# Attention pipeline with its steps set further apart, transposes alternating between two whole PSUM banks

## The chip, the cores and the metric

The kernel runs on one core of one Trainium2 chip. The metric is the device time of one execution in microseconds (us). The engines are named as the profile names them: PE is TensorE, PEld its weight load, DVE VectorE, ACT ScalarE, POOL GpSimd and SP SyncE.

## The reference

One layer of a decoder over 256 tokens of width 2048, all in float32. The part that matters here is the attention and the projections on either side of it:

```python
h = rms_norm(x, mix_norm_g)
q, kv, gate_logits, conv_in = split(h @ w_in)          # 16 query heads, 4 key/value heads, head size 64
# three branches, each a softmax over logits + T5 bias, each weighted by a sigmoid gate:
#   compressed: keys/values squeezed to 15 blocks by a small MLP
#   selected:   top-16 blocks of 64 (all 4 blocks here, so all causal keys)
#   window:     last 512 keys (all causal keys here)
attn = g0 * o_cmp + g1 * o_sel + g2 * o_win
conv = conformer_conv(conv_in)                          # GLU, 31 taps, LayerNorm, swish
x = x + concat([attn, conv]) @ w_out
x = x + conv_glu_ffn(rms_norm(x))                       # 2048 -> 2 x 5632 -> 2048, 3 taps
return rms_norm(x, final_norm_g)
```

## The kernel before, in words

Every float32 product of weights is computed as three products of rounded parts: a weight chunk (128 x 2048) arrives in `wraw`, ACT rounds it into `wh` (line 110), DVE or POOL forms the rest `wl` (line 115), and PE adds high x high, high x low and low x high in PSUM (`mm3`, lines 144 to 146, for the input projections; `mm_rows`, lines 151 to 153, for the output projections).

The order of the instructions on each engine is the order in which the program is written. While PE works on a chunk, `hook` is called four times at even distances. It may call `attn_tick`, then runs what stands in `behind`, issues one piece of the next weight split (`w_pump`), and runs one entry of the list `steps`.

The input projection ends with eight tiles of queries (`i` = 0 to 7, 48 `mm3` matmuls each, in bank 0 or 1 by turns). When a tile is done, `q_evac` (line 659, DVE) scales it, and `q_split` splits it into a high half (line 665, ACT) and a low half (line 666, DVE). Behind it runs a software pipeline over 32 units; unit n is one pair (head slot, branch), four units to a query tile, and odd and even units share one score product. One call of `attn_tick` is one tick and issues each step for a different unit:

- `st_scores`: PE, logits of two units (lines 732 and 733), into bank 2 and bank 4 or 5
- `st_min`: DVE, adds the bias, writes `e` and its minimum `mn` (line 742)
- `st_exp`: ACT, exponential of `e` with sums into `lsum` (line 753)
- `st_rec`: DVE, reciprocal and gate (lines 761 and 762), once for two units
- `st_scale`: POOL, scales `e` (line 768)
- `st_transpose`: PE, three 128 x 128 transposes of `e` into bank 6 (line 774)
- `st_evac`: ACT, copies bank 6 to `es` (line 779)
- `st_out`: PE, every fourth unit, the products with the values into the lower half of bank 7 (lines 794 and 797); ACT then rounds the result to `ma_h` (line 798) and DVE forms `ma_l` (line 799)

The table at line 815 says how many ticks back the unit of each step lies: scores 0, min 1, exp 1, reciprocal and scale 3, transposes and eviction 5, output 6. Within a tick the steps are issued in the order of the table.

The compressed branch runs beside it from the list `steps`, for two query tiles at a time: `cmp_scores` (PE, line 678, bank 3), `cmp_exp` (DVE lines 688 to 692, ACT line 693), `cmp_probs` (DVE lines 698 to 701), `cmp_tr` (PE, two transposes at line 706 in bank 3 again, ACT copy to `pct` at line 708).

The first tick falls into query tile 1; tiles 2 to 7 have four ticks each, and 12 of the 38 ticks fall into the first three of the 16 chunks of the output projection, which reads `ma_h` and `ma_l`. From there to the end PE runs the rest of the output projection, the up projection (lines 1000 and 1002) and the down projection.

## Time and profile before

| | us |
|---|---|
| median of three runs (1119.32 to 1121.04) | 1120.76 |
| profiled execution | 1119.51 |
| its span, first to last instruction | 1117.7 |
| PE busy | 1098.8 |
| DVE busy | 768.4 |
| ACT busy | 577.0 |
| POOL busy | 187.8 |

The profiled execution is one run with its own time; its span is 1.8 us shorter, which lies before the first and after the last instruction. Busy times are sums over the whole span, so they say nothing about a single stage. In an order of time a number after an instruction says how long its engine had stood idle just before it, and the arrow names what ended that.

### The profile page before, as it was taken

How to read it: one execution, taken by the hardware profiler on the slowest of the kernel's cores; microseconds unless marked ns; L12 is line 12 of the kernel's file. 1: busy time of each engine (PE TensorE's matmuls, PEld its weight loads, DVE VectorE, ACT ScalarE, POOL GpSimd, SP SyncE). 2: the span in 40 equal slices, each digit the busy share in tenths (PEclk: the TensorE clock that was granted, in tenths of full speed). 3: DMA queues.
4: the chain of work that ended last, by engine and by line, in shares of the span. 5: the costliest groups of instructions: out<-in, count | busy, mean ns of one | idle time of the engine just before them, and what ended most of it. 6: DMA issues, size and time to landing. Idle time of an engine off the chain costs nothing.

```text
span 1117.7 us, 16341 instructions
## 1 busy us (share of the span) xinstructions
PE 1098.8 (98%) x6530; PEld 957.2 (86%) x6530; DVE 768.4 (69%) x1255; ACT 577.0 (52%) x833; POOL 187.8 (17%) x143
## 2 busy tenths in 40 slices
PE   8999999998999999999999999999999999999997
PEld 8999999886788888888888888888888888888885
DVE  7899976766356677777777777777778655556554
ACT  7534456777645554555455555545555444444442
POOL 0888756666100000000000000000000000000000
PEclk9999999999999999999999999999999999999999
DMA  9685426222464655555555555555555555555542
GB/s 375 235 294 198 170 79 246 94 80 86 175 226 155 230 188 196 188 193 191 192 191 194 190 190 190 189 188 189 188 189 189 189 188 188 189 183 188 186 158 76
DMA packets 32425, 207.46 MB, mean 186 GB/s; under 512 B 3883, under 2 KB 6203, under 8 KB 8284
## 3 DMA queue, kind: packets, MB, share of 16 engines
q1 hardware_dynamic: 28972, 199.85, 49.9%
q10 hardware_dynamic: 3376, 6.55, 1.6%
q8 instruction: 51, 0.84, 0.3%
q14 instruction: 26, 0.21, 0.1%
HBM read 204.27 MB, written 2.12 MB: 185 GB/s over the span
## 4 chain that ended last, share of the span: by engine, by line
PE 92%; DVE 2%; ACT 2%; issue 1%; DMA 1%; POOL 1%; SPq 0%; POOLq 0%; DVEq 0%; ACTq 0%
PE bank L1000 29%; PE bank L1002 14%; PE bank L153 10%; PE bank L151 9%; PE bank L152 9%; PE bank L144 5%; PE bank L146 5%; PE bank L145 5%; PE bank L794 1%; DVE wl L115 1%; DMA hb<-in_head 1%; POOL e L768 1%; ACT wh L110 1%; ACT e L753 1%; PE bank L774 0%
## 5 line engine op out<-in xcount | busy, mean ns | idle before, releaser
L110 ACT ACTIVATE wh<-wraw 128x2048 fp32r<-128x2048 f32 (+2 forms) x239 | 355.6, 1505 | 366.7 <-issue 149.8
L115 DVE TENSOR_TENSOR wl<-wraw,wh 128x2048 fp32r<-128x2048 f32 (+1 forms) x185 | 363.9, 1973 | 197.2 <-ACT wh L110 197.1
L1000 PE MATMUL bank<-xt,wh 128*128 128x512 f32 x1408 | 488.7, 394 | 0.0
L1002 PE MATMUL bank<-xt,wl 128*128 128x256 f32 x1408 | 390.1, 277 | 0.0
L1000 PEld LDWEIGHTS bank<-xt,wh 128*128 128x128 f32 x1408 | 264.0, 188 | 61.2
L1002 PEld LDWEIGHTS bank<-xt,wl 128*128 128x128 f32 x1408 | 264.4, 188 | 0.0
L144 PE MATMUL bank<-xt,wh 128*128 128x256 f32 x512 | 146.8, 287 | 1.6 <-ACT wh L245 1.6
L146 PE MATMUL bank<-xt,wl 128*128 128x256 f32 x512 | 145.1, 283 | 0.3 <-DVE wl L246 0.2
L145 PE MATMUL bank<-xt,wh 128*128 128x256 f32 x512 | 144.8, 283 | 0.0
L152 PE MATMUL bank<-wl,gh 128*128 128x512 f32 (+1 forms) x360 | 140.8, 391 | 0.0
L151 PE MATMUL bank<-wh,gh 128*128 128x512 f32 (+1 forms) x360 | 140.8, 391 | 0.0
L153 PE MATMUL bank<-wh,gl 128*128 128x512 f32 (+1 forms) x360 | 140.8, 391 | 0.0
L180 POOL TENSOR_TENSOR rstd<-ms,half 128x1 f32<-128x1 f32 x4 | 2.2, 552 | 821.4 <-DVE ms L173 821.4
L115 POOL TENSOR_TENSOR wl<-wraw,wh 128x1024 fp32r<-128x1024 f32 (+1 forms) x54 | 121.4, 2284 | 31.0 <-ACT wh L110 27.3
L144 PEld LDWEIGHTS bank<-xt,wh 128*128 128x128 f32 x512 | 97.7, 191 | 3.5 <-ACT wh L245 2.1
L146 PEld LDWEIGHTS bank<-xt,wl 128*128 128x128 f32 x512 | 97.8, 191 | 0.7 <-DVE wl L246 0.7
L145 PEld LDWEIGHTS bank<-xt,wh 128*128 128x128 f32 x512 | 97.8, 191 | 0.4
L375 DVE SCALAR_TENSOR_TENSOR bank<-us,cw,bank 128x256 f32<-128x256 f32 x232 | 93.9, 481 | 2.0 <-ACT bank L370 1.6
L963 DVE SCALAR_TENSOR_TENSOR yt<-u,vecs,yt 128x255 f32<-128x255 f32 (+1 forms) x176 | 80.9, 480 | 3.1
L151 PEld LDWEIGHTS bank<-wh,gh 128*128 128x128 f32 x360 | 67.8, 188 | 15.8
L152 PEld LDWEIGHTS bank<-wl,gh 128*128 128x128 f32 x360 | 67.8, 188 | 15.8
L153 PEld LDWEIGHTS bank<-wh,gl 128*128 128x128 f32 x360 | 67.8, 188 | 15.8
(182 smaller groups left out, 1034.1 us busy)
## 6 DMA issues: line engine op xcount, KB each, us to landing
wraw<-in_w_u SPq DMA_DIRECT2D x88, 1024.0 KB, 4.8
wraw<-in_w_d SPq DMA_DIRECT2D x44, 1024.0 KB, 4.8
wraw<-in_w_t SPq DMA_DIRECT2D x30, 1024.0 KB, 5.1
wraw<-in_w_o SPq DMA_DIRECT2D x16, 1024.0 KB, 4.8
wraw<-in_w_vg SPq DMA_DIRECT2D x4, 608.0 KB, 3.9
hb<-in_head SPq DMA_DIRECT2D x2, 1024.0 KB, 9.7
xr<-in_x SPq DMA_DIRECT2D x2, 1024.0 KB, 19.1
wb<-rel_scratch ACTq DMA_DIRECT2D x1, 2048.0 KB, 10.3
```

The lines of the kernel that those rows point to most:

```text
L110: nc.scalar.activation(h[:, sl], raw[:, sl], AF.Copy)
L115: (nc.gpsimd if pooled else nc.vector).tensor_sub(l[:, sl], raw[:, sl], h[:, sl].bitcast(F32))
L144: nc.tensor.matmul(ps, wh, xh, start=first, stop=False)
L145: nc.tensor.matmul(ps, wh, xl, start=False, stop=False)
L146: nc.tensor.matmul(ps, wl, xh, start=False, stop=last)
L151: nc.tensor.matmul(ps, xh, wh, start=first, stop=False)
L152: nc.tensor.matmul(ps, xh, wl, start=False, stop=False)
L153: nc.tensor.matmul(ps, xl, wh, start=False, stop=last)
L375: nc.vector.scalar_tensor_tensor(y[:, j] if last else acc[0], us[:, j, k:k + T], cw[:, j, k:k + 1], acc[0], op0=OP.mult, op1=OP.add)
L963: nc.vector.scalar_tensor_tensor(ys[i][:, d:], us_[i][:, :T - d], fcw[:, c, k:k + 1], ys[i][:, d:], op0=OP.mult, op1=OP.add)
L1000: nc.tensor.matmul(bk[i], wh[:, k, sl], xt[:, kt].rearrange("p a t -> p (a t)"), start=kt == 0, stop=False)
L1002: nc.tensor.matmul(bk[i][:, :T], wl[:, k, sl], xt_h[:, kt], start=False, stop=kt == KD - 1)
```

## The change

Ticks: a unit's exponential is now issued two ticks after its scores instead of one, reciprocal and scale four ticks instead of three, the transposes six instead of five, the eviction `es` seven instead of five, the output product eight instead of six. The rounding of the output, which stood in the same tick as the output product, becomes two steps: `st_high` (ACT) one tick after it and `st_low` (DVE) two ticks after it; only the last unit has both at once.

Banks: the transposes of even units go to bank 3, of odd units to bank 6. The compressed branch leaves bank 3: its logits go to bank 1 and its transposes to bank 0, which are the query banks not being filled at that moment; for the last two query tiles, which fall into the output projection, to the upper half of bank 7 and to bank 5.

Queries: `q_split` issues the high half only; the low half (`q_low`) runs at the next hook. Ticks in the output projection are dealt out again: 40 ticks in all, 14 of them after the query tiles. `e` has six buffers instead of five and `es` five instead of four; two small tiles share the buffers of others.

```diff
-            if not side:
-                while behind:
-                    behind.pop(0)()
+            due, first = behind[:], not side
+            behind.clear()
+            for f in due if first else ():
+                f()
             w_pump(1)
             step()
             fill(1.0 if i in ticks else 0.8 if cbst["q"] else 2.0)
-            while behind:
-                behind.pop(0)()
+            for f in () if first else due:
+                f()
...
-            cf["d"] = wk.tile([P, 2, P], F32, name="dg", bufs=1)
+            cf["d"] = wk.tile([P, 2, P], F32, name="dg", tag="sg")
...
-            cm[kv] = hd = wk.tile([P, 4, 32], F32, name="hd")
+            cm[kv] = hd = wk.tile([P, 4, 32], F32, name="hd", tag="q32")
...
         def q_split(i):
             for r in range(2):
+                h = slice(64 * r, 64 * r + 64)
+                nc.scalar.activation(qs[h, i % 4, r], q32[i][h], AF.Copy)
+            behind.append(lambda: q_low(i))
+
+        def q_low(i):
+            for r in range(2):
                 h, o = slice(64 * r, 64 * r + 64), slice(64 - 64 * r, 128 - 64 * r)
-                nc.scalar.activation(qs[h, i % 4, r], q32[i][h], AF.Copy)
                 nc.vector.tensor_sub(qs[o, i % 4, r], q32[i][h], qs[h, i % 4, r].bitcast(F32))
...
-            cm["b"] = bank[3]
+            cm["b"] = bank[1] if m < 3 else bank[7][:, T:]
...
-            pg = cm["b"]
+            pg = bank[0] if m < 3 else bank[5]
...
-                        (cmp_scores, cmp_exp, lambda m: None, cmp_probs, cmp_tr))]
+                        (lambda m: None, cmp_scores, cmp_exp, cmp_probs, lambda m: None, cmp_tr))]
...
-            e = wk.tile([P, 384], F32, name="e", bufs=D_T)
+            e = wk.tile([P, 384], F32, name="e", bufs=6)
...
+        def st_pt(n):
+
+            return bank[6 if n % 2 else 3][:, :384]
+
         def st_transpose(n):
-            e = US[n][0]
-            pt = bank[6]
+            e, pt = US[n][0], st_pt(n)
...
-            es = wk.tile([P, 384], F32, name="es", bufs=4)
-            nc.scalar.activation(es, bank[6][:, :384], AF.Copy)
+            es = wk.tile([P, 384], F32, name="es", bufs=5)
+            nc.scalar.activation(es, st_pt(n), AF.Copy)
...
-            nc.scalar.activation(ma_h[:, i], bank[7][:, :T], AF.Copy)
-            nc.vector.tensor_sub(ma_l[:, i], bank[7][:, :T], ma_h[:, i].bitcast(F32))
+            if n == NU - 1:
+                st_high(n)
+                st_low(n)
+
+        def st_high(n):
+            if n % 4 == 3:
+                nc.scalar.activation(ma_h[:, n // 4], bank[7][:, :T], AF.Copy)
+
+        def st_low(n):
+            if n % 4 == 3:
+                nc.vector.tensor_sub(ma_l[:, n // 4], bank[7][:, :T], ma_h[:, n // 4].bitcast(F32))
...
-        DEEP = D_T + 1
+        DEEP = 8
...
-            for f, d in ((st_out, DEEP), (st_transpose, D_T), (st_scores, 0), (st_rec, D_S), (st_min, 1),
-                         (st_evac, D_T), (st_scale, D_S), (st_exp, 1)):
-                if 0 <= n - d < NU:
+
+            for f, d in ((st_out, DEEP), (st_transpose, 6), (st_scores, 0), (st_low, 10), (st_rec, 4), (st_min, 1),
+                         (st_evac, 7), (st_high, 9), (st_scale, 4), (st_exp, 2)):
+                if 0 <= n - d < NU - (f in (st_high, st_low)):
...
-        TICKS = {0: {}, 1: {2: 1, 3: 1}, 2: {0: 1, 1: 1, 2: 1, 3: 1}, 3: {0: 1, 1: 2, 2: 1, 3: 2}, 4: {1: 1, 2: 1, 3: 2}}
+        TICKS = {0: {}, 1: {2: 1, 3: 1}, 2: {0: 1, 1: 1, 2: 1, 3: 1}, 3: {0: 1, 1: 1, 2: 2, 3: 2}, 4: {0: 1, 1: 1, 2: 1}}
...
-                    hook(2 * t + k // 2, TICKS[(3, 4, 2)[min(n, 2)]])
+                    hook(2 * t + k // 2, TICKS[(3, 2, 4)[min(n, 2)]])
```

ACT's order in query tile 5, before: `qs` is the high half of the queries, `wh` a weight piece, `es` the eviction of the transposes, `e` the exponentials, `pct` the compressed branch, `ma_h` the rounded output (bank_67 is bank 3, bank_70 bank 6, bank_71 bank 7).

```order
L665 ACTIVATE qs<-q_2840 64x256 x2
L110 ACTIVATE wh<-wraw 128x1024
L779 ACTIVATE es<-bank_70 128x384
L753 ACTIVATE e,lsum<-e,mn 128x128
L753 ACTIVATE e,lsum<-e,mn 128x256
L110 ACTIVATE wh<-wraw 128x1024
L779 ACTIVATE es<-bank_70 128x384
L753 ACTIVATE e,lsum<-e,mn 128x128
L753 ACTIVATE e,lsum<-e,mn 128x256
L708 ACTIVATE pct<-bank_67 128x256
L798 ACTIVATE ma_h<-bank_71 128x256
L779 ACTIVATE es<-bank_70 128x384
```

ACT's order from the same point of the same query tile now (bank_64 is bank 0).

```order
L666 ACTIVATE qs<-q_2814 64x256 x2
L110 ACTIVATE wh<-wraw 128x1024
L789 ACTIVATE es<-bank_67 128x384
L760 ACTIVATE e,lsum<-e,mn 128x128
L760 ACTIVATE e,lsum<-e,mn 128x256
L110 ACTIVATE wh<-wraw 128x1024
L789 ACTIVATE es<-bank_70 128x384
L814 ACTIVATE ma_h<-bank_71 128x256
L760 ACTIVATE e,lsum<-e,mn 128x128
L760 ACTIVATE e,lsum<-e,mn 128x256
L715 ACTIVATE pct<-bank_64 128x256
L789 ACTIVATE es<-bank_67 128x384
```

The kinds and the number of instructions are the same; the eviction now reads the two banks by turns, and it is for a unit that was transposed a tick earlier. `ma_h` has moved from the tick of its output product to the next one.

DVE's order at the same hand-over of query tiles, before: `ma_l` is the low half of the output, `q` the evicted query tile, `qs` its low half.

```order
L799 TENSOR_TENSOR ma_l<-bank_71,ma_h 128x256
L761 RECIPROCAL lsum<-lsum 128x4
L762 TENSOR_TENSOR lsum<-lsum,gates 128x4
L742 ISA e,mn<-bank_66,wb 128x128
L742 ISA mn 128x1
L742 ISA e,mn<-bank_68,wb 128x256
L742 ISA mn 128x1
L115 TENSOR_TENSOR wl<-wraw,wh 128x1024
L659 SCALAR_TENSOR_TENSOR q_2988<-bank_65,rB 128x256
```

DVE's order from that query tile on, now.

```order
L660 SCALAR_TENSOR_TENSOR q_2962<-bank_65,rB 128x256
L768 RECIPROCAL lsum<-lsum 128x4
L769 TENSOR_TENSOR lsum<-lsum,gates 128x4
L749 ISA e,mn<-bank_66,wb 128x128
L749 ISA mn 128x1
L749 ISA e,mn<-bank_68,wb 128x256
L749 ISA mn 128x1
L749 ISA e,mn<-bank_66,wb 128x128
L749 ISA mn 128x1
L749 ISA e,mn<-bank_69,wb 128x256
L749 ISA mn 128x1
L672 TENSOR_TENSOR qs<-q_2962,qs 64x256 x2
```

Before, `qs` stood behind the first of the two minima of this piece and ahead of reciprocal and gate; now it stands behind both minima and behind reciprocal and gate. `ma_l` now stands two ticks behind the output product, ahead of a minimum.

PE's order at the third hook of the first output chunk, now: two ticks are issued there at once (L784 are the transposes, L739 and L740 the logits).

```order
L153 MATMUL bank_65<-wh,ma_l 128x512
L784 MATMUL bank_67<-ident,e 128x128 x3
L739 MATMUL bank_66<-k_h,qs 128x256
L740 MATMUL bank_66<-k_l,qs 128x256
L739 MATMUL bank_68<-k_h,qs 128x512
L740 MATMUL bank_68<-k_l,qs 128x512
L784 MATMUL bank_70<-ident,e 128x128 x3
L151 MATMUL bank_65<-wh,ma_h 128x512
```

Before, both groups of transposes at such a hook went to bank_70, so the second had to follow the eviction of the first.

## Rows read from the trace of the kernel before

**Rows 1.** Page, part 1: busy us (share of the span) xinstructions.

```profile
PE 1098.8 (98%) x6530; PEld 957.2 (86%) x6530; DVE 768.4 (69%) x1255; ACT 577.0 (52%) x833; POOL 187.8 (17%) x143
```

**Rows 2.** Waits of TensorE: us in total, times, longest us.

```profile
PE bank L774 <- ACT es L779: 4.5, 5, 1.7
...
PE bank L774 <- POOL e L768: 1.3, 3, 0.6
PE bank L706 <- DVE pcb L701: 1.2, 1, 1.2
...
PE bank L678 <- DVE q L659: 0.2, 1, 0.2
```

**Rows 3.** Stretches: two query tiles, output stage with pipeline, output stage after it.

```profile
core 0: us, PE busy (x) PEld busy (x) DVE busy (x) ACT busy (x) POOL busy (x), PEclk, DMA share, GB/s
...
230.10:253.20 23.10, 22.47 (x189) 20.12 (x187) 15.49 (x61) 17.70 (x53) 14.46 (x17) 1.00 0.28 96
260.00:293.00 33.00, 28.56 (x175) 20.13 (x174) 16.06 (x62) 20.12 (x57) 19.16 (x21) 1.00 0.38 134
293.00:366.00 73.00, 73.00 (x327) 59.01 (x326) 40.22 (x42) 39.05 (x56) 0.00 (x0) 1.00 0.51 186
```

**Rows 4.** TensorE in order of time: start, length, instruction [idle before <-releaser].

```profile
205.96 0.28 PE L146 MATMUL bank<-xt,wl 128*128 128x256 f32 x1
207.93 0.52 PE L774 MATMUL bank<-ident,e 128*128 128x128 f32 x3 [1.69 <-ACT es L779]
208.37 0.38 PE L732 MATMUL bank<-k_h,qs 128*128 128x256 f32 x1
...
214.49 0.28 PE L146 MATMUL bank<-xt,wl 128*128 128x256 f32 x1
214.62 0.49 PE L774 MATMUL bank<-ident,e 128*128 128x128 f32 x3
214.86 0.37 PE L732 MATMUL bank<-k_h,qs 128*128 128x256 f32 x1
...
219.98 0.37 PE L732 MATMUL bank<-k_h,qs 128*128 128x256 f32 x1
...
224.17 0.55 PE L774 MATMUL bank<-ident,e 128*128 128x128 f32 x3
```

**Rows 5.** ScalarE in order of time ahead of the wait at 207.93.

```profile
204.59 0.40 ACT L753 ACTIVATE e<-e,mn 128x128 f32<-128x128 f32 x1 [1.65 <-DVE mn L742]
...
205.49 0.84 ACT L665 ACTIVATE qs<-q 64x256 fp32r<-64x256 f32 x2
206.35 1.06 ACT L110 ACTIVATE wh<-wraw 128x1024 fp32r<-128x1024 f32 x1
207.31 0.47 ACT L779 ACTIVATE es<-bank 128x384 f32<-128x384 f32 x1
```

**Rows 6.** Waits of all engines, three that the two moved evictions and e cause.

```profile
DVE ma_l L799 <- ACT ma_h L798: 21.6, 8, 7.0
...
ACT e L753 <- DVE mn L742: 12.7, 20, 1.7
...
DVE qs L666 <- ACT qs L665: 7.6, 8, 1.0
```

**Rows 7.** VectorE in order of time, query tiles 3 and 4.

```profile
213.32 0.42 DVE L799 TENSOR_TENSOR ma_l<-bank,ma_h 128x256 fp32r<-128x256 f32 x1 [1.84 <-ACT ma_h L798]
...
217.62 0.86 DVE L666 TENSOR_TENSOR qs<-q,qs 64x256 fp32r<-64x256 f32 x2 [1.02 <-ACT qs L665]
...
222.59 0.35 DVE L688 TENSOR_TENSOR ec<-bank,wb 128x28 f32<-128x28 f32 x2
```

**Rows 8.** GpSimd in order of time: scales of e, end of the pipeline.

```profile
271.69 7.50 POOL L768 TENSOR_SCALAR e<-e,lsum 128x128 f32<-128x128 f32 x8 [3.38 <-DVE lsum L762]
282.95 4.84 POOL L768 TENSOR_SCALAR e<-e,lsum 128x128 f32<-128x128 f32 x4 [3.77 <-DVE lsum L762]
```

**Rows 9.** VectorE ahead of the last scales.

```profile
282.05 0.42 DVE L799 TENSOR_TENSOR ma_l<-bank,ma_h 128x256 fp32r<-128x256 f32 x1 [3.68 <-ACT ma_h L798]
```

More of the change, by code (lines that the diff above doesn't have):

```diff
@@ L292, in tab_rel @@
             nc.tensor.matmul(pr[:16, :384], rbn, oh[:, P:], start=True, stop=True)
-            rtab = wk.tile([16, 384], F32, name="rtab", tag="e", bufs=5)
+            rtab = wk.tile([16, 384], F32, name="rtab", tag="e", bufs=6)
             nc.vector.tensor_copy(rtab, pr[:16, :384])
@@ L797, in st_out @@
                 nc.tensor.matmul(o[r], vc[:, i % 2, i // 4, r], pct[:, i // 2], start=False, stop=True, **kw)
-            nc.scalar.activation(ma_h[:, i], bank[7][:, :T], AF.Copy)
-            nc.vector.tensor_sub(ma_l[:, i], bank[7][:, :T], ma_h[:, i].bitcast(F32))
+            if n == NU - 1:
[7 more added lines that the diff above has]
+                nc.vector.tensor_sub(ma_l[:, n // 4], bank[7][:, :T], ma_h[:, n // 4].bitcast(F32))
         tick = {"n": 0}
         NU = len(units)
-        D_S, D_T = 3, 5
-        DEEP = D_T + 1
+        DEEP = 8
         HALVES = ((0, P, P), (P, 384, 0))
```

## The prediction, written before the changed kernel ran

> **What bounds the kernel now.** I read the engine totals first: PE is busy 1098.8 of 1117.7 us [rows 1], so all that any change of order can win is PE's idle time. The head of the kernel, where the first weights arrive, and the tail behind the last matmul are not touched by this change. That leaves the stretch in which the attention pipeline runs. Apart from the head, the list of PE's waits holds hardly anything that is not in it: 4.5 us in five waits of the transposes for the eviction `es`, 1.3 us in three waits of the transposes for POOL's scaled `e`, 1.2 us in one wait of the compressed transposes for DVE, 0.2 us of the compressed logits for a query tile [rows 2]. Together 7.2 us in ten waits. The table of stretches shows the same from outside: PE is busy 28.56 of 33 us while the output projection carries the rest of the pipeline, and 73 of 73 us once the pipeline has drained [rows 3]. So time saved in the pipeline is not lost again at once, and PE's granted clock is at its full level (1.00, which is 2.4 GHz) in all of these stretches, so no clock is to be won.
>
> A wait costs more than the idle time beside it. Undisturbed, the last `mm3` matmul starts at 214.49, the transposes at 214.62 and the scores at 214.86: 0.37 us. Around the longest wait the same three start at 205.96, 207.93 and 208.37: 2.41 us, so 2.04 us are lost where the row shows 1.69 us idle [rows 4]. The rest, 0.35 us, is the end of a matmul that counts as busy and a slower restart. With 0.35 us for each of nine waits (the tenth is only 0.2 us long) the waits cost 7.2 + 3.2 = 10.4 us. That is the ceiling.
>
> Why the transposes wait is seen on ACT. Between 204.59 and 207.78 ACT runs two exponentials, the high half of a query tile, a weight piece of 1.06 us and only then the eviction, and this chain began 1.65 us late because the exponentials waited for DVE's minimum [rows 5]. In the whole stage ACT waits 12.7 us for minima of the same tick, and DVE waits 21.6 us in eight waits for `ma_h`, because `ma_l` stands in the tick of its own output product [rows 6]. While DVE waits there it does not run the minima behind it, ACT then gets those late, and PE the evictions late. The same in the drain: DVE stood 3.68 us before the `ma_l` at 282.05 [rows 9], the reciprocal is behind it, so POOL started its last scales only at 282.95 after 3.77 us of idling [rows 8], and PE waited for them.
>
> **The change part by part.** No matmul, eviction or vector operation is added or removed; PE's work is the same.
>
> Two transposing banks and the eviction one tick later: an eviction had to lie between the end of its own transposes and the next transposes, one tick. Two query tiles (eight ticks) take 23.10 us [rows 3], so a tick is 2.9 us, and the chain above takes 3.2 us. Now the eviction has from the end of the tick before to the start of the tick after, two ticks or some 5 us. The longest chain fits. Saved: the five waits, 4.5 + 5 x 0.35 = 6.2 us. The ticks are not short of ACT: ACT is busy 17.70 of 23.10 us there, DVE 15.49, POOL 14.46 [rows 3]. With PE 1 us faster over two tiles ACT would have 17.7 us of work in 22.1 us, so it still keeps up.
>
> `st_high` and `st_low` in ticks of their own, and the exponential two ticks behind the scores: DVE's 21.6 us and ACT's 12.7 us of waiting [rows 6] are not PE's time, so they count nothing by themselves. What they give is that the minima, sums and scales come earlier, and with them the three POOL waits and the compressed wait (the latter also has one more hook between its probabilities and its transposes in the last pair). Saved: 1.3 + 1.2 us and four times 0.35 us, 3.9 us, if all of it goes, and 0.2 us for the query tile, since the last compressed logits are issued one hook later. 6.2 + 3.9 + 0.2 is 10.3 us, the ceiling but for rounding.
>
> Against that stand new waits. The low half of a query tile is issued a hook later, behind two minima. Before it ended at 217.62 + 0.86 = 218.48 us and PE used it at 219.98 [rows 4, 7]: 1.5 us to spare. One minimum and the reciprocal pair now stand ahead of it, about 1.0 us of DVE work, but its 1.02 us wait for ACT is gone and so is the 1.84 us wait of `ma_l` just before [rows 7]. I take nothing for it; what it costs if that cover fails is a rival below. The compressed logits now lie in a query bank that PE refills at the next tile. DVE read them at 222.59 to 222.94 [rows 7]; PE's next tile began some 1.0 us after the transposes at 224.17 (their 0.3 us and six matmuls of 0.12 us) [rows 4]. That leaves 2.2 us, and DVE gets earlier. Nothing, with a bound of 1.2 us, the one wait for that branch [rows 2], for each of three such tiles. The buffers of `e` and `es` grow by one as the distances grow by one, so they free as before or a tick earlier. No DMA moves to another queue, and the loads of `x2` on ACT's queue stay at the third output chunk.
>
> Where ticks come in pairs, POOL is the slow one: four units took 7.50 us [rows 8], 1.88 us each, and two pairs and a single tick follow each other across the first two output chunks. PE's 28.56 us over twelve ticks [rows 3] are 2.4 us a tick on the average; a pair shares the weight matmuls of one hook, so I put a tick of this burst at 1.5 us, an estimate. Five ticks then give POOL 7.5 us for five units, which need 9.4 us. The two ticks between scale and transposes, as many as before, cover most of the 1.9 us. Between 0 and the present three POOL waits, 1.3 + 3 x 0.35 = 2.4 us, I take 1.0 us, below the middle because POOL's late start came from `ma_l`.
>
> The sum: 10.4 - 1.0 = 9.4 us. The profiled execution of before would come to 1119.5 - 9.4 = 1110.1 us. It lies 1.25 us below the median of the three runs; the four times average 1120.2, and from that I forecast **1110.8 us**.
>
> One page speaks against it. TensorE: Matmul & The Clock Gate, section "HAM oscillation — how this bites in real kernels", in the Trainium skill, reports a thin matmul kernel in which PSUM double-buffering gave no further gain (126.6 against 125.5 us). By it the second transposing bank would be worth nothing, which is the third rival below. The row at 207.93, a wait for an eviction of the only bank, says that here the bank is waited for.
>
> **The rivals.** *The output stage keeps its waits.* There the compressed logits now share bank 7 with the output product, so the product of unit 23 must follow DVE's read of those logits, which is issued only a hook before it, behind a minimum and a weight piece, and POOL is short in the bursts. The trace gives 33 us to that stage with 4.4 us idle [rows 3]. If only the query tiles gain, that is the 1.69 us wait [rows 4] and 0.63 us in each of the last two pairs of tiles (23.10 - 22.47) [rows 3], with 0.35 us for each, 4.0 us go and the time is 1116; if half of the other 6.4 us goes too, 1113. For it: the burst and the new order of banks. Against it: DVE has 16.06 us of work in these 33 us. PSUM — Partial Sum Buffer, section "PSUM bank collisions raise a hardware error", in the Trainium skill, says that two engines must be kept apart by bank, not by address; no row of before shows such a pair in bank 7.
>
> *Slower.* PE waits at the scores of each query tile for the low half that is now a hook later. It hits seven tiles. It has to eat 9.4 us and 2.2 us more to count as slower, 1.7 us a tile, so DVE would have to come 1.5 + 1.7 = 3.2 us later at this point than before, although 2.9 us of its waits go there. If it did by 3.5 us, seven waits of 2.0 us cost 14 us: 1125 us.
>
> *No change.* ACT is as late with two banks as with one, because the chain of 3.2 us comes again at each query tile and is followed by more of the same. Then the transposes wait for ACT whatever the bank, and the time is 1120.2. For it: only 5.4 us of 23.1 are free on ACT. Against it: those 5.4 us were mostly spent waiting for things of the same tick.
>
> **How the numbers follow.** Most waits go (1109 to 1113, residual waits of 0 to 2.4 us and the scatter of 0.9 us around the median): 0.68. The output stage keeps half or more of its waits (1113 to 1117): 0.17. No change: 0.09. Slower: 0.06. A change of 0.2%, 2.2 us, is about what runs of this kernel can tell from none. Faster is the first two, 0.85. The range goes from 1108.5 (no wait left, lowest run) to 1116.5; it leaves out the last two cases and a little of the second.
>
> **What would show it.** Right: PE's waits in the stage down from 7.2 to about 1 us, none for `es`; two query tiles in about 22.1 instead of 23.1 us; `ma_l` and the exponentials without waits; what is left is for POOL's `e` in the output stage. Wrong: a wait of PE's scores for DVE at each query tile, a wait at the start of a query tile or at the product in bank 7, or weight matmuls that wait for `wh` or `wl`, which nothing in before does.

## Result and profile after

The changed kernel takes 1111.05 us (median of four runs, 1110.87 to 1111.36) against 1120.16 us (four runs of the kernel before, 1119.32 to 1121.04). The ratio is 0.9919, with a 95% interval of 0.9902 to 0.9936. The profiled execution took 1111.1 us with a span of 1109.3 us; against the profiled execution of before that is 8.4 us less.

The engine totals, to be held against [rows 1]: the same work counts 2.3 us less as busy on PE.

```profile
PE 1096.5 (99%) x6530; PEld 957.0 (86%) x6530; DVE 768.5 (69%) x1255; ACT 574.3 (52%) x833; POOL 183.7 (17%) x143
```

The waits of TensorE in 186 to 366 us (us in total, times, longest us), which answer to [rows 2]. Lines have moved: the transposes are now L784, the eviction L789, the output products L804.

```profile
PE bank L784 <- ACT es L789: 0.8, 3, 0.4
...
PE bank L784 <- POOL e L775: 0.2, 1, 0.2
PE bank L804 <- ACT es L789: 0.2, 1, 0.2
```

Ten waits of 7.2 us have become five of 1.2 us. These 6.0 us and the 2.3 us of busy time are the 8.4 us, but for rounding. So a wait did cost more than its idle time, roughly 2.3 us over all where 9 x 0.35 = 3.2 were put down; roughly, because PE's busy time also differs by 2.0 us (1095.6 to 1097.6) among the kernels below that have no wait longer than 0.6 us in these 180 us. The gain lies in the stage of the pipeline: from the first scores to the first matmul of the up projection it took 182.72 us (189.20 to 371.92) and takes 174.37 us (189.25 to 363.62). The stretches answer to [rows 3]; the first is the whole stage of the query tiles, the second one is two of them, from one group of transposes to the same group two tiles on.

```profile
186.00:260.00 74.00, 73.05 (x594) 66.53 (x596) 54.99 (x204) 57.13 (x168) 42.58 (x53) 1.00 0.34 122
222.82:245.25 22.43, 22.27 (x187) 20.09 (x187) 15.39 (x61) 17.02 (x53) 13.48 (x17) 1.00 0.26 95
260.00:293.00 33.00, 32.83 (x200) 24.92 (x196) 15.48 (x47) 21.13 (x53) 14.15 (x18) 1.00 0.42 162
```

The first of these stretches in the kernel before:

```profile
186.00:260.00 74.00, 70.92 (x583) 64.44 (x583) 50.69 (x187) 55.38 (x157) 41.78 (x49) 1.00 0.31 110
```

PE idled 3.08 us in the query tiles and 4.44 us in the output stage; now it is 0.95 and 0.17 us. Two query tiles take 22.43 us, where they took 23.10 and 22.1 were forecast. Of the three stops of ScalarE and VectorE that answer to [rows 6] little is left: DVE waits for `ma_h` in two places, both in the output stage, 2.07 us and, at the last unit, 7.28 us; ACT waits 0.8 us once for a minimum, and DVE 0.5 us once for `qs`. VectorE stands longer than before for the scores themselves (12.4 us in five places, before 2.3 us in three).

What is left was not foreseen. ScalarE in order of time in query tile 4 of the changed kernel (start, length, instruction, idle time before it):

```profile
221.99 0.30 ACT L700 ACTIVATE ec<-ec 128x120 f32<-128x120 f32 x1 [3.96 <-DVE ec L699]
222.20 0.47 ACT L789 ACTIVATE es<-bank 128x384 f32<-128x384 f32 x1
```

and the transposes that wait for it:

```profile
222.82 0.52 PE L784 MATMUL bank<-ident,e 128*128 128x128 f32 x3 [0.16 <-ACT es L789]
```

ACT stood 3.96 us in front of the exponential of the compressed branch, and the eviction was queued behind it. The same picture comes again at 245.25. The longest wait that is left is another one, 0.45 us at 206.10, at the place of the long wait of [rows 4].

### The profile page after: what moved, and what is told of

The parts are those of the page before. It is cut to its first block, busy times and chain, and to the rows that moved or that the text cites. A ratio compares the mean times of both kernels' runs of the same rounds, so it can differ in the third digit from the quotient of the medians.

```text
span 1109.3 us, 16328 instructions
## 1 busy us (share of the span) xinstructions
PE 1096.5 (99%) x6530; PEld 957.0 (86%) x6530; DVE 768.5 (69%) x1255; ACT 574.3 (52%) x833; POOL 183.7 (17%) x143
## 4 chain that ended last, share of the span: by engine, by line
PE 94%; DVE 2%; ACT 1%; DMA 1%; issue 1%; POOL 0%; SPq 0%; DVEq 0%; POOLq 0%; ACTq 0%
PE bank L1019 29%; PE bank L1021 15%; PE bank L153 10%; PE bank L151 10%; PE bank L152 10%; PE bank L144 5%; PE bank L146 5%; PE bank L145 5%; PE bank L804 1%; PE bank L784 1%; DMA hb<-in_head 1%; DVE wl L115 1%; PE bank L533 0%; PE bank L639 0%; PE bank L637 0%
```

## The experiments

The medians of the kernel before lie between 1119.4 and 1120.8 us beside the different experiments (the last section gives the likely reason), so each ratio is against the runs of before that were taken beside the same experiment; it is a ratio of means, not of medians. The idle times are PE's in 186 to 260 us and in 260 to 293 us, the same windows for all, so a faster kernel has done more of its work in them. The stage is the time from the first scores to the first matmul of the up projection in the profile; in experiments 4 and 5 it holds 1.7 us of a lower clock (last section).

| kernel | us, median | ratio, 95% interval | idle, query tiles | idle, output stage | stage |
|---|---|---|---|---|---|
| before | 1120.16 | 1 | 3.08 | 4.44 | 182.72 |
| changed | 1111.05 | 0.9919 (0.9902 to 0.9936) | 0.95 | 0.17 | 174.37 |
| 1 one bank | 1110.80 | 0.9913 (0.9900 to 0.9927) | 1.05 | 0.09 | 174.30 |
| 2 two banks, eviction in its tick | 1110.23 | 0.9908 (0.9895 to 0.9922) | 0.64 | 0.42 | 173.51 |
| 3 halves joined | 1113.28 | 0.9936 (0.9924 to 0.9948) | 1.16 | 1.57 | 176.68 |
| 4 exponential one tick back | 1112.17 | 0.9928 (0.9915 to 0.9940) | 2.15 | 0.17 | 176.74 |
| 5 two banks alone | 1120.86 | 1.0002 (0.9993 to 1.0011) | 3.89 | 4.56 | 184.31 |
| 6 low half of queries joined | 1110.87 | 0.9913 (0.9897 to 0.9928) | 1.05 | 0.18 | 174.39 |
| 7 compressed exponential later | 1109.33 | 0.9899 (0.9886 to 0.9913) | 0.62 | 0.00 | 172.80 |
| 8 parts of 1, 3 and 4 undone | 1113.75 | 0.9941 (0.9929 to 0.9953) | 2.32 | 1.74 | 177.29 |
| 9 split of the halves alone | 1116.50 | 0.9970 (0.9958 to 0.9982) | 2.70 | 3.12 | 179.89 |
| 10 steps a tick later alone | 1117.38 | 0.9969 (0.9956 to 0.9981) | 0.65 | 4.61 | 179.31 |
| 11 one bank and 7 | 1110.51 | 0.9912 (0.9899 to 0.9926) | 0.78 | 0.57 | 174.11 |
| 12 ticks as before | 1110.21 | 0.9914 (0.9900 to 0.9928) | 1.02 | 0.00 | 173.66 |

### 1. One transposing bank

```diff
-            return bank[6 if n % 2 else 3][:, :384]
+            return bank[6][:, :384]
...
-                         (st_evac, 7), (st_high, 9), (st_scale, 4), (st_exp, 2)):
+                         (st_evac, 6), (st_high, 9), (st_scale, 4), (st_exp, 2)):
```

> The changed kernel, but all transposes go through bank 6 again and each eviction is issued in the tick of its transposes; every other distance stays as changed. The prediction's theory (two banks and the later eviction are worth 6.2 us by themselves, because a transposing step waits until ScalarE has evicted the step before): PE waits for es again in front of most transposing steps of the output of the query tiles, some 5 us in all, and the time is 1116 to 1118 us. Rival (the other distances keep ScalarE early enough that one bank would do): 1111 to 1112 us, and PE waits for es no longer than the 1.0 us in four waits that the changed kernel shows.

It took 1110.8 us, as fast as the changed kernel and a little below the rival's range. TensorE's waits in this kernel:

```profile
PE bank L784 <- ACT es L789: 0.9, 3, 0.4
...
PE bank L784 <- POOL e L775: 0.2, 1, 0.2
```

The 6.2 us that the forecast gave to the second bank and the later eviction do not come back as a loss; the rival is right.

### 2. Two banks, eviction in the tick of its transposes

The second line of the diff of experiment 1 alone (`st_evac` 6).

> The changed kernel with its two transposing banks, but each eviction is issued in the tick of its transposes instead of one tick later. This splits the 6.2 us that the prediction gave to both together. If the second bank alone does it (a transposing step then waits for the eviction two steps back, which has a whole tick): 1111 to 1112 us, es waits of PE under 1.5 us. If the later issue does it (an eviction that stands in ScalarE's queue ahead of the exponentials holds them up until PE has transposed): 1114 to 1117 us, with waits of PE for POOL's e or for es of 3 us and more.

1110.2 us, 0.8 us less than the changed kernel: the later eviction isn't needed either. PE waits for no `es` at all, but 0.6 us for `e` and 0.4 us for a low half of queries.

### 3. `ma_h` and `ma_l` joined behind the output products

```diff
-            if n == NU - 1:
-                st_high(n)
-                st_low(n)
+            st_high(n)
+            st_low(n)
```

The two entries of the table of steps are taken out.

> The changed kernel, but ma_h and ma_l are issued at once behind the output products of a query tile, as before, instead of one and two ticks later. The prediction's theory gives the split of the two, with the later exponential, 3.9 us: DVE again stands some 2.5 us in front of each ma_l and what is queued behind it is late, and the time is 1112.5 to 1115 us, with waits of PE for POOL's e or for pcb back. Rival (with the exponentials and the reciprocals a tick later there is slack enough for DVE's stop): 1111 to 1111.6 us, DVE's wait for ma_h back at 20 us but nothing of it on PE.

1113.3 us, 2.2 us more than the changed kernel. In the pipeline's stretch (186 to 295 us) DVE's wait for `ma_h` is back:

```profile
DVE ma_l L817 <- ACT ma_h L813: 26.0, 8, 5.9
```

and PE idles 1.57 us in the output stage, 0.53 and 0.57 us of it for POOL's `e` and 0.47 us at the compressed logits for `ma_l`. In the query tiles little changed (1.16 against 0.95 us idle). So this part does what the forecast said, in the stage that it said. The wait of 0.47 us is not one of before, though: the changed kernel has put the logits of the last pair into the bank that `ma_l` reads.

### 4. Exponential one tick behind the scores

`(st_exp, 2)` becomes `(st_exp, 1)`.

> The changed kernel, but the exponential is issued one tick behind the scores, in the tick of its minima, as before (reciprocal, scaling, transposes and evictions keep the changed distances). The prediction's theory (the exponential's wait for DVE's minimum stands in ScalarE's queue ahead of evictions, but two banks cover it): ScalarE's wait for mn back at 10 to 13 us, PE's waits up by 0 to 1 us, 1111 to 1112.2 us. Rival (the exponential's distance is what took the waits for POOL's e and es away): 1114 us or more.

1112.17 us as a median, but five runs from 1111.58 to 1113.32: two at 1113.07 and 1113.32 with a mean granted clock of 0.996, three at 1111.58 to 1112.17 with 0.997 to 0.999. The profile is of one of the two. It has one long wait, 1.82 us of the transposes for `es`, the one of [rows 4] again, in spite of two banks and the later eviction. ScalarE and TensorE at that place:

```profile
203.71 0.40 ACT L760 ACTIVATE e<-e,mn 128x128 f32<-128x128 f32 x1 [2.40 <-DVE mn L749]
...
206.43 0.47 ACT L789 ACTIVATE es<-bank 128x384 f32<-128x384 f32 x1
```

```profile
207.05 0.64 PE L784 MATMUL bank<-ident,e 128*128 128x128 f32 x3 [1.82 <-ACT es L789]
```

The chain of [rows 5] is back: the exponential waits for its minimum, and behind it stand the query's high half, a weight piece and the eviction. The time fits the first forecast, and ScalarE's wait for `mn` is back, at 16.2 us above its 10 to 13. What failed is its reason, that two banks cover this wait.

### 5. Two banks and the new place of the compressed branch alone

The kernel before with the bank lines of the change; steps at 0, 1, 3, 5 and 6 ticks, eviction in the tick of its transposes.

> The kernel before with the two transposing banks and the compressed branch in the query banks alone: all distances of the steps, the ticks per hook, the joined ma_h and ma_l and the order of the low half of the queries are those of before. The prediction's theory (a second bank takes a transposing step off the eviction just ahead of it; the 6.2 us counted it with the later eviction): 1114 to 1116.5 us, the five es waits of PE gone or short, its waits for POOL's e and for pcb still there or longer. Rival (a second bank by itself buys nothing while ScalarE is as late as before, because its queue is held up by ma_h, minima and early evictions): 1119.5 to 1120.5 us.

1120.86 us, ten of eleven runs at 1120.7 to 1121.0 and one at 1119.4 us: nothing gained. The waits of TensorE show what became of the five for `es`:

```profile
PE bank L739 <- DVE mn L749: 3.9, 3, 2.2
PE bank L784 <- POOL e L775: 2.3, 5, 0.7
...
PE bank L713 <- DVE mn L749: 1.8, 1, 1.8
```

In order of time, at the place of the long wait of [rows 4]:

```profile
205.61 0.49 PE L784 MATMUL bank<-ident,e 128*128 128x128 f32 x3
208.30 0.36 PE L739 MATMUL bank<-k_h,qs 128*128 128x256 f32 x1 [2.20 <-DVE mn L749]
```

The transposes start at once, since their bank is free, and the scores right behind them wait 2.20 us for the minimum that has to empty their own bank. DVE gets to that minimum only at 207.86, after it had stood 1.02 us before the low half of the queries and done the probabilities of the compressed branch. The bank was one gate; the next one, 0.2 us further on, was as late. Not all of the rival's reason holds, though: it spoke of ScalarE, and PE now waits for VectorE.

### 6. Low half of the queries in its old hook

`behind.append(lambda: q_low(i))` becomes `q_low(i)`.

> The changed kernel, but DVE's subtraction for the low half of the queries stands directly behind ScalarE's qs in the same hook, as before. The prediction took this edit at nothing on PE: DVE waits some 7 us in eight places for qs again, and the time is 1111 to 1111.6 us. Rival (DVE's stop there delays the minima and so the exponentials and evictions): 1112 to 1113.5 us, with more waits of PE for es or POOL's e than the 1.2 us of the changed kernel.

1110.87 us, no difference; PE gets one new wait of 0.2 us. The forecast's nothing for this edit holds. VectorE's stop of some 7 us that I expected did not come back: it waits 0.5 us for `qs`. In the kernels with the exponential at one tick in which it is joined (before and experiments 5 and 9) it waits 7.6 to 7.9 us, and 3.1 us in experiment 10 with the exponential at two, so most of this stop came from ACT's high half standing behind late exponentials.

### 7. The compressed branch's exponential one step later

```diff
-            nc.scalar.activation(e, e, AF.Exp, scale=-1.0)
+
+        def cmp_exp2(m):
+            nc.scalar.activation(cm["e"], cm["e"], AF.Exp, scale=-1.0)
...
-                       ((lambda m: None, cmp_scores, cmp_exp, lambda m: None, cmp_probs, lambda m: None, cmp_tr) if m < 3 else
-                        (lambda m: None, cmp_scores, cmp_exp, cmp_probs, lambda m: None, cmp_tr))]
+                       ((lambda m: None, cmp_scores, cmp_exp, cmp_exp2, cmp_probs, lambda m: None, cmp_tr) if m < 3 else
+                        (cmp_scores, cmp_exp, cmp_exp2, cmp_probs, lambda m: None, cmp_tr))]
```

> The changed kernel, but the compressed branch's exponential on ScalarE is issued one step behind DVE's subtraction ahead of it instead of in the same step. In the changed kernel ScalarE stands 4.0 and 4.2 us in front of that exponential, with an eviction queued behind it, and the transposes two ticks later start 0.3 us late in each of two places, and once the output products 0.2 us late. Theory (that queue place is the cause of these waits): the waits at these places are gone, 1110.2 to 1110.8 us. Rival (the eviction was late for PE's transposes and not for the queue): the same waits stay, 1111 to 1111.4 us.

1109.33 us (1109.32 to 1109.38), the fastest kernel of all, 1.7 us under the changed kernel and 0.9 us under the range that I expected. Two query tiles between the same groups of transposes, and the output stage:

```profile
222.27:244.34 22.07, 22.07 (x188) 20.06 (x187) 15.36 (x61) 17.36 (x53) 13.34 (x17) 1.00 0.28 97
260.00:293.00 33.00, 33.00 (x199) 25.20 (x196) 15.74 (x47) 22.20 (x55) 13.94 (x16) 1.00 0.44 160
```

PE doesn't idle in either, and the pair of tiles takes the 22.1 us that the forecast had put down. ScalarE's order ahead of the transposes at 222.27 shows the reason:

```profile
218.63 0.49 ACT L791 ACTIVATE es<-bank 128x384 f32<-128x384 f32 x1 [0.82 <-PE bank L786]
...
221.76 0.30 ACT L702 ACTIVATE ec<-ec 128x120 f32<-128x120 f32 x1 [1.52 <-DVE ec L699]
221.97 0.47 ACT L791 ACTIVATE es<-bank 128x384 f32<-128x384 f32 x1
```

An eviction and two exponentials now run while ACT used to stand in front of `ec`. The wait of 0.45 us at the place of [rows 4] is still there (at 205.88), so it has another cause, which stays open. From the transposes at 245.25 (here 244.34) to the last output product the time fell from 40.22 (285.47 - 245.25) to 39.34 us (283.68 - 244.34). The waits shown there account for less than half of these 0.9 us; for the last pair of tiles the logits also stand one hook earlier, and the rest isn't settled.

### 8. Three parts undone together

The edits of experiments 1, 3 and 4 in one kernel.

> The changed kernel with three parts undone together: one transposing bank with eviction in its tick, ma_h and ma_l joined behind the output products, exponential one tick behind the scores. What stays is the reciprocal and scaling at 4, transposes at 6, output products at 8, the new ticks per hook and the later low half of the queries. Undone one by one the three cost -0.2, 2.4 and 1.3 us against the 1110.9 of the changed kernel. Theory A (ScalarE's stops at mn and DVE's stops at ma_l were one chain that made es late, and either cure is enough for most of it): the two together cost far more than their sum, 1116.5 to 1120 us, with PE's waits for es at 3 us and more again. Theory B (the extra tick between scaling, transposes and output products is what lets PE through): about additive, 1113.5 to 1115 us.

1113.75 us, in the range of theory B: about additive, and no chain that closes again shows. The 1.3 us that the expectation took for experiment 4 hold the lower clock of two of its runs; with the three others (median 1111.79) the exponential costs some 0.7 us, the halves cost 2.2 us and the bank nothing, and 2.7 us is what the three together cost here. The long wait is back with one bank as it was with two in experiment 4:

```profile
207.08 0.52 PE L784 MATMUL bank<-ident,e 128*128 128x128 f32 x3 [1.81 <-ACT es L789]
...
275.97 0.52 PE L784 MATMUL bank<-ident,e 128*128 128x128 f32 x3 [1.00 <-POOL e L775]
```

This kernel says the most about the sum of the forecast. The banks, the later eviction, the split of the halves and the exponential's second tick are all taken out, and still its stage takes 177.29 us, where before took 182.72 and changed takes 174.37 us: 5.4 of the 8.3 us remain.

### 9. The split of the halves alone, in the kernel before

`st_high` and `st_low` of the change, and this table (a line of bounds is left out):

```diff
-            for f, d in ((st_out, DEEP), (st_transpose, D_T), (st_scores, 0), (st_rec, D_S), (st_min, 1),
-                         (st_evac, D_T), (st_scale, D_S), (st_exp, 1)):
+            for f, d in ((st_out, DEEP), (st_transpose, D_T), (st_scores, 0), (st_low, DEEP + 2), (st_rec, D_S), (st_min, 1),
+                         (st_evac, D_T), (st_high, DEEP + 1), (st_scale, D_S), (st_exp, 1)):
```

> The kernel before with one part alone: ma_h one tick and ma_l two ticks behind the output products, nothing else. Theory A (DVE's 21.6 us of stops at ma_l make the minima late, these the exponentials, these the evictions): half of the gain or more, 1113 to 1116 us, es waits of PE under 2 us. Theory B (the steps need a tick more between them and the stops hardly matter): 1118 to 1120.5 us, with es waits of PE still 3 us and more.

1116.5 us (four runs at 1116.2 to 1116.6, two at 1117.9 and 1118.0), between the two forecasts: 0.30% faster, yet 3.8 us of waits for `es` in six places remain, the long one of 1.69 us unchanged. DVE's wait for `ma_h` is 7.6 us in two places. The gain lies in the output stage (3.12 us idle instead of 4.44), and a little of it in the waits at the later pairs of tiles (0.63 us each before, 0.18 for `es` and 0.25 for `mn` now).

### 10. Steps a tick later alone, with one bank

The kernel of experiment 5 with one bank and the table of steps at exponential 2, reciprocal and scale 4, transposes and eviction 6, output 7.

> The kernel before with exponential, reciprocal and scaling, transposes with their eviction, and output products one tick later each (2, 4, 6, 7 instead of 1, 3, 5, 6), one transposing bank, ma_h and ma_l joined, the ticks per hook and the low half of the queries as before; the compressed branch is in the banks of the queries. Against it the changed kernel with joined halves (1113.3 us) has output products one tick later still, other ticks per hook and the later low half. Theory B (the tick between the steps does it): 1112.5 to 1115 us. Theory A (DVE's stops at ma_l stay and keep everything late): 1116 us or more.

1117.38 us as a median of two runs at 1116.0 and three at 1117.4, between the theories. The two stretches tell them apart:

```profile
186.00:260.00 74.00, 73.35 (x601) 66.73 (x601) 54.45 (x199) 55.63 (x163) 42.65 (x51) 1.00 0.35 125
260.00:293.00 33.00, 28.39 (x171) 20.27 (x171) 15.32 (x51) 19.13 (x51) 16.55 (x20) 1.00 0.34 128
```

The query tiles are cured (0.65 us idle, 0.45 of it at the place of the long wait) with one bank and with the halves joined; the output stage is as bad as before (4.61 us). Why the first is so, ScalarE shows at the place of [rows 5]:

```profile
204.53 1.06 ACT L110 ACTIVATE wh<-wraw 128x1024 fp32r<-128x1024 f32 x1
205.50 0.47 ACT L789 ACTIVATE es<-bank 128x384 f32<-128x384 f32 x1
205.87 0.39 ACT L760 ACTIVATE e<-e,mn 128x128 f32<-128x128 f32 x1
```

The exponentials no longer stand ahead of the query's high half with a wait of 1.65 us, and the eviction starts at 205.50 instead of 207.31. Why the second is so, three engines show in the output stage of the same kernel, all in order of time. VectorE:

```profile
279.86 0.42 DVE L817 TENSOR_TENSOR ma_l<-bank,ma_h 128x256 fp32r<-128x256 f32 x1 [5.97 <-ACT ma_h L813]
280.20 0.17 DVE L768 RECIPROCAL lsum<-lsum 128x4 f32<-128x4 f32 x1
```

GpSimd, whose scales wait for that reciprocal and the gate behind it:

```profile
280.76 3.95 POOL L775 TENSOR_SCALAR e<-e,lsum 128x128 f32<-128x128 f32 x3 [4.29 <-DVE lsum L769]
```

And TensorE, whose transposes wait for the scaled `e`:

```profile
283.28 0.33 PE L784 MATMUL bank<-ident,e 128*128 128x128 f32 x1 [1.68 <-POOL e L775]
```

DVE stands 5.97 us in front of `ma_l`, the reciprocal is queued behind it, POOL idles 4.29 us, PE 1.68 us: the chain of [rows 8, 9].

### 11. One bank and the later compressed exponential

The edits of 1 and 7 together.

> The changed kernel with one transposing bank, eviction in the tick of its transposes, and the compressed branch's exponential one step later. If the second bank has no part in the gain at all: 1109.3 to 1110.3 us, as with two banks and the same later exponential (1109.3), waits of PE in the stage under 1 us. If two banks matter once ScalarE's queue is clear: 1110.5 to 1111.5 us with more es waits than the one of 0.4 us.

1110.51 us (1110.41 to 1110.65), 1.2 us more than experiment 7. PE waits for `es` 1.1 us in two places instead of 0.4 us in one. So beside the later compressed exponential the two banks with the later eviction are worth about 1 us after all; this is the only pair of kernels in which they show, and why they do so only here is not shown.

### 12. The ticks per hook as before

```diff
-        TICKS = {0: {}, 1: {2: 1, 3: 1}, 2: {0: 1, 1: 1, 2: 1, 3: 1}, 3: {0: 1, 1: 1, 2: 2, 3: 2}, 4: {0: 1, 1: 1, 2: 1}}
+        TICKS = {0: {}, 1: {2: 1, 3: 1}, 2: {0: 1, 1: 1, 2: 1, 3: 1}, 3: {0: 1, 1: 2, 2: 1, 3: 2}, 4: {1: 1, 2: 1, 3: 2}}
...
-                    hook(2 * t + k // 2, TICKS[(3, 2, 4)[min(n, 2)]])
+                    hook(2 * t + k // 2, TICKS[(3, 4, 2)[min(n, 2)]])
```

and the edit of experiment 6.

> The changed kernel with the ticks per hook of the output projection as before (two ticks at the second and at the fourth hook of the first chunk, the single ticks of the two chunks behind it exchanged) and the low half of the queries back in its old hook, which by itself cost nothing (1110.9 us). All distances, the split of ma_h and ma_l and the two banks stay. This tells what keeps the 33 us stretch of the output projection without waits. Theory C (the dealing out of the ticks does it: the late steps with the ticks of before still idled 4.6 us there, with the new ticks and output products a tick later 1.6 us): 1113.5 to 1116 us, PE's waits for POOL's e back at 2 us and more. Rival (the larger distance to the output products and the split do it, whatever the ticks): 1110.8 to 1112 us.

1110.21 us and no idle time in the output stage: with the halves split, dealing out the ticks anew was not needed.

## Why the prediction was right, and for the wrong part of the change

The time, the direction and the forecast of about 1 us left in PE's waits were right. The sum behind them was not: its largest term measured nothing, and 5.4 of the 8.3 us gained in the stage remain when all the parts that it priced, but for the order of the last compressed pair, are taken out. That the total came out all the same is partly luck. The ceiling of 10.4 us was counted from the waits themselves, so any cure that took most of them away would have met it, whichever part was credited.

**Two transposing banks and the eviction one tick later: 6.2 us.** This step failed. Without them the time is the same (experiment 1), with them alone nothing is gained (experiment 5). The working set an eviction's one tick of 2.9 us against a chain of 3.2 us, but that chain began 1.65 us late [rows 5]. The same rows named that wait, and it was the thing to price. The long wait of [rows 4] follows the exponential's distance and not the banks: with the exponential at two ticks 0.45 us of it are left with two banks (changed) and 0.44 to 0.45 us with one (experiments 1 and 10); with the exponential at one tick it is 1.82 us with two banks (experiment 4) and 1.81 us with one (experiment 8). The page "TensorE: Matmul & The Clock Gate" of the Trainium skill, section "HAM oscillation — how this bites in real kernels", with its double-buffering that gave nothing, was weighed and set aside because a row showed a wait for the only bank. The outcome agrees with the page here (ratio 1.0002 for the banks alone). The reason here is that a wait for a bank says which gate closed last, not that a second bank opens the way. Experiment 5 shows the next gate 0.2 us behind the first.

**Halves and exponential: 3.9 + 0.2 us.** The mechanism holds, the size was too large by what taking them back costs: 2.2 us for the halves (experiment 3), some 0.7 us for the exponential (experiment 4), 2.7 us for both with the banks (experiment 8). The halves act in the output stage, as forecast. The exponential acts in the query tiles, on the wait that the forecast had given to the banks.

**Reciprocal and scaling, transposes and output products a tick or two later: no term.** The sum priced these distances only as buffers and as cover for POOL, and the new order of the last compressed pair at no more than the 1.2 + 0.35 us of the compressed transposes' wait and 0.2 us of its logits'. Experiment 8 keeps all of these and has none of the parts above, and 5.4 of the 8.3 us remain. From the other side, experiment 10 (exponential, scaling, transposes and output products one tick later) gains 3.4 us: the query tiles are cured, the output stage is not (4.61 us idle), nor does the split alone cure it (3.12 us, experiment 9). Output products at 8 ticks with the new order of the last compressed pair bring 1.57 us with the halves joined (experiment 3), and the split on top of it 0.17. The parts overlap, so what each is worth depends on which others are there. Which of the two, the eighth tick or the order of that pair, does its share in the output stage was not separated. For the order speaks that the wait of the compressed transposes, 1.2 to 1.8 us, stands in the four kernels with the old order (before, 5, 9 and 10) and in none with the new. The ticks per hook do nothing with the halves split (experiment 12); with them joined that was not tried.

**New waits taken at nothing.** The later low half of the queries costs nothing (experiment 6). The compressed branch in the query banks makes no tile wait, but the branch wasn't free: its exponential holds ScalarE's queue for 4 us, and the evictions behind it are late. "None for `es`" was therefore wrong: four such waits remain, three of the transposes and one of the output products, 1.0 us together, and all but the 0.45 us at 206.10 are gone in experiment 7. At 222.82 the transposes start 0.44 us behind the start of the matmul ahead of them instead of 0.12, so 0.32 us are lost there, and as much at 245.25: the 22.43 instead of 22.1 us for two tiles. Experiment 7 gives these back; its span, 1107.5 us, is 10.2 us under that of before, and the forecast's ceiling was 10.4.

**The residual of 1.0 us for POOL in bursts.** POOL was not short: one wait of 0.2 us. About as much as the residual was lost at `es` instead.

**From the sum to the forecast.** The sum gave 1110.1 us for the profiled execution; it took 1111.1, so the gain was 8.4 and not 9.4 us. The 0.7 us added for the median of before made up for most of that. "No clock is to be won" was right for the profile and wrong for the runs, as the last section shows. Of the rivals, the output stage's waits did not stay and nothing got slower; the third one's outcome came true for the banks alone.

## What to carry to other kernels

Before a second buffer is credited with a wait, look at what its releaser did before it: when that engine's queue began late because of a wait for a value of the same tick, move that consumer a tick away first, since the buffer may only shift the stop to the next instruction, as in experiment 5. In a software pipeline on engines that take their instructions in order, search each queue for an instruction that waits and has due work behind it: here the exponential at `mn` (some 0.7 us when put back), `ma_l` (2.2 us) and the exponential of `ec` (1.7 us). Cure each in the stage in which it shows, for two cures that each look partial may be needed together.

## Not expected of the hardware

TensorE's granted clock fell after single waits of about 2 us, in some executions. Kernel of experiment 5, PE idle from about 206.1 to 208.3 (columns as in the stretches; the granted clock is the third figure from the end):

```profile
207.00:208.00 1.00, 0.00 (x0) 0.00 (x0) 0.90 (x6) 0.61 (x2) 0.00 (x0) 1.00 0.02 8
208.00:209.00 1.00, 0.70 (x4) 0.68 (x5) 1.00 (x5) 0.81 (x4) 0.89 (x2) 1.00 0.00 0
209.00:210.00 1.00, 1.00 (x9) 0.92 (x7) 1.00 (x4) 1.00 (x3) 1.00 (x2) 0.76 0.00 0
210.00:211.00 1.00, 1.00 (x6) 1.00 (x6) 1.00 (x3) 1.00 (x5) 1.00 (x2) 0.50 0.00 0
211.00:212.00 1.00, 1.00 (x7) 0.78 (x7) 0.32 (x1) 0.64 (x3) 1.00 (x1) 0.50 0.00 0
212.00:213.00 1.00, 1.00 (x8) 0.62 (x8) 0.00 (x0) 0.00 (x0) 0.11 (x1) 0.54 0.00 0
213.00:214.00 1.00, 1.00 (x16) 0.68 (x12) 0.00 (x0) 0.00 (x0) 0.00 (x0) 1.00 0.00 0
```

The clock goes from 2.4 to 1.2 GHz while PE is busy again, and is back at 2.4 by 213; by these rows (0.24 + 0.50 + 0.50 + 0.46) 1.7 us are lost. The profile of experiment 4 shows the same after its wait of 1.82 us; that of experiment 8, after 1.81 us at the same place, stays at 1.00:

```profile
208.00:209.00 1.00, 1.00 (x5) 0.70 (x5) 0.90 (x6) 1.00 (x3) 0.67 (x2) 0.50 0.00 0
...
208.00:209.00 1.00, 1.00 (x10) 0.91 (x9) 0.97 (x6) 1.00 (x2) 0.64 (x2) 1.00 0.00 0
```

The runs of experiment 4 fall into two groups by time and clock, so the clock falls in some executions of a kernel and not in others. That would explain the scatter of before: of its 43 runs beside the experiments 15 lie at 1119.16 to 1119.77 us with a mean granted clock of 0.997 or 0.998, and 28 at 1120.68 to 1121.32 us with 0.996. No profile of a run of the second group was taken, so that the fall sits at the wait of 1.69 us is inferred from experiments 4 and 5. Experiment 10, with a wait of 1.68 us, has two such groups too (0.997 and 0.996). Experiment 9, with 1.69 us, has two groups of times, but their mean clocks (0.997 to 0.998 and 0.997) hardly tell them apart, and experiment 8 has one group in five runs. Against the first group the changed kernel gains about 8.3 us, as in the profiles; the rest of the difference of the medians would be the clock, and the changed kernel, without a long wait, has one group only.
